# The first feed-forward of a hybrid encoder gets a group of seven products in its fourth chunk; row sums earlier, position tables and convolution diagonals later

## The chip, the cores and the metric

The kernel runs on one core of one Trainium2 chip. The metric is device time in microseconds from start to end of one execution, lower is better. The engines are named as in the profile: PE is TensorE's matmul, PEld its weight load, DVE VectorE, ACT ScalarE, POOL GpSimd, SP SyncE, which issues nearly all DMAs.

## The reference

Two layers over 256 tokens of width 1024, in float32. Each layer is half a feed-forward, a mixer, half a feed-forward; the mixer is a convolution module in layer 0 and latent attention in layer 1. At the end stands one more norm. So there are four feed-forwards, in this order: first (ahead of the convolution), second (behind it), third (ahead of the attention), fourth.

```python
def swiglu_ffn(h, w1, w3, w2):                      # 1024 -> 2816 -> 1024
    return (jax.nn.silu(h @ w1) * (h @ w3)) @ w2

for i in range(2):
    h = h + 0.5 * swiglu_ffn(rmsnorm(h, ffn_norm1[i]), ffn1_w1[i], ffn1_w3[i], ffn1_w2[i])
    m = rmsnorm(h, mix_norm[i])
    h = h + (conv_module(m, ...) if i == 0 else mla(m, positions, ...))
    h = h + 0.5 * swiglu_ffn(rmsnorm(h, ffn_norm2[i]), ffn2_w1[i], ffn2_w3[i], ffn2_w2[i])
return rmsnorm(h, final_norm)
```

Attention turns its keys and queries by `cos` and `sin` of position times frequency (the position tables). The convolution has 31 taps for each channel.

## The kernel before

**Precision.** A float32 product is made of three matmuls of a faster type: each operand is split into a high half (a cast, `hi`, on ACT) and a low half (the rest, `lo`, on DVE), and `mm3` (L330) adds high x low, high x high and low x high. In the profile these are L332, L335 and L336, named `u` in the first product of a feed-forward and `o` in the second.

**Weights.** All weights are cut into blocks of 128 x 2048 (1024 KB), in one list `blocks` in the order of use. `load` fetches a block into one of four `raw` buffers (SP queue), casts it in two pieces (L246) and makes its low half in two pieces (L247), into one of five `hi`/`lo` pairs. `load_ahead` runs up to three or four blocks ahead of the one in use. A `raw` buffer comes free when both low pieces are made, a `hi`/`lo` pair when TensorE has read it.

**A feed-forward** (`ffn_in`). The first product goes over 2816 columns in chunks `c` = 0 to 5: five of 512 columns, four blocks each (two for `w1`, two for `w3`), and one of 256 columns with two blocks. Two row tiles `tb` of 128 tokens, eight k tiles. After each chunk comes the activation and the multiplication (L953, L955), the result `s` is turned by a DMA through DRAM (`turn_blocks`, L475 to L484), and cast into `Gh` and `Gl` (L850). The second product goes over eleven blocks of `w2`.

**Groups of seven.** `seven_products` multiplies a 2 x 2 arrangement of blocks by seven products in place of eight, after Winograd: four blocks of weights become seven sums and differences, made on the way (`load_seven`: four subtractions of 128 x 2048 on DVE, L200; casts L214), and the rows need four sums too (`sums_of_rows`, L344; split by `forms_of`, L361 and L364). Where the rows are those of the normed input, `whole_rows` (L349) first adds their high and low halves into a tile `xs`, which takes a `raw` buffer. The products run in the order j = 0 to 6 into four PSUM banks; between them the banks are copied and added (L258): ACT copies bank `c11` to `c21` after product 0, and product 2 adds to `c21`.

`SEVEN_DOWN = (0, 1, 2, 3)`: the second product of all four feed-forwards begins with such a group. `SEVEN_UP = {1: (3,), 2: (3,), 3: (3,)}`: the first product of the second, third and fourth feed-forward has one in chunk 3. The row sums for it are made in chunk `min(seven_up) - 2`, or `- 1` where the rows come whole from the start (`X.whole`, only the first feed-forward, where it did not apply).

**The first feed-forward.** `first_rows` splits the input and the first two blocks as they arrive. The products of chunk 0 are L408. Beside it, `beside()` steps a generator `diagonals` that writes 63 convolution diagonals of 128 x 64 (`dpair`, and later `rows`, L1676) on ACT. The row sums' tile `rows4` is also used for the diagonals of the other half, which wait until the second product's row sums have been read.

**Position tables.** `rope_tables` (L1357 and on) makes them of 21 small operations on DVE and four sines on ACT. It is called late in the program, just ahead of the attention.

**Order.** A scheduler puts each engine's instructions in an order; `order(a, b)` makes a stand behind b on its engine with no wait, `urgent` raises a priority, `behind` keeps casts behind the last urgent instructions of their engine. What has no such tie the scheduler places by its own estimate: in the built kernel the position tables stand on DVE among chunk 1's blocks, and 31 diagonals on ACT stand there too. On each engine the instructions then run in that order.

**The norm ahead of the convolution** (`Plain`) loads the sigmoid's table on ACT (L666) ahead of the convolution's gates.

Of the kernel before, what the change touches and what calls it, by code (L numbers as in the profile page):

```python
# [19 lines left out]
P = 128  # L20
# [22 lines left out]
PIECES = 2  # L43
# [2 lines left out]

SEVEN_UP = {1: (3,), 2: (3,), 3: (3,)}
SEVEN_DOWN = (0, 1, 2, 3)  # L50

CONV_DVE = (0, 2, 4)
# [37 lines left out]
def trunk(ctx: ExitStack, tc: tile.TileContext, x, xt, first, pos, invf, gfin, wdw,  # L90
# [244 lines left out]
        nc.tensor.matmul(o, ah, bh, start=False, stop=False, skip_group_check=seeded)  # L335
        return nc.tensor.matmul(o, al, bh, start=False, stop=stop, skip_group_check=seeded)  # L336

    def sums_of_rows(x11, x12, x21, x22):


        sums = [(0, x22, x21, x22, ALU.add), (2, x21, x11, x21, ALU.subtract), (1, x11, x22, x11, ALU.subtract),
                (3, x12, x12, x11, ALU.subtract)]
        for n, out, left, right, op in sums:
            nc.vector.tensor_tensor(out, left, right, op=op)  # L344
        return sorted(((n, out) for n, out, *_ in sums), key=lambda s: s[0])

    def whole_rows(xh, xl):
# [20 lines left out]
    def seven_products(xh, xl, forms, banks, late={}):  # L368


        def rows(a, tb):
            k = slice(4 * a, 4 * a + 4)
            return xh[:, k, tbs(tb)], xl[:, k, tbs(tb)]

        def product(a, b, fresh):
            load_ahead(W_BUFS - 1)
            (hi, lo), = weights(1, False)
            for k in range(4):
                c = slice(k * 512, k * 512 + 512)
                before[:] = [mm3(b, a[0][:, k], a[1][:, k], hi[:, c], lo[:, c], fresh and k == 0, k == 3, before, True)]  # L380

        n0 = n_used[0]
        before = []
        c11, c21, c12, c22 = banks[0, 0], banks[1, 0], banks[0, 1], banks[1, 1]
        product(rows(0, 0), c11, True)
        first = urgent(nc.scalar.copy)(c21, c11)
        for cast in late.values():
            order(cast, first.ins)
        product(forms[0], c22, True)
        kept = tmp.tile([P, 512], F32, tag="s", name=uid("p5"))  # L390
        last = urgent(nc.scalar.copy)(kept, c22)
        product(forms[1], c21, False)
        add = urgent(nc.vector.tensor_add)(c12, c21, kept)
        order(casts[n0 + 5, 0][1], add.ins)
        for high, low in gates[-NT:] if not late else ():
            order(high, last.ins)
            order(low, add.ins)
        product(rows(1, 0), c11, False)
        product(forms[2], c21, False)
        add = urgent(nc.vector.tensor_add)(c22, c21, kept)  # L400
        order(casts[n0 + 6, 0][1], add.ins)
        product(forms[3], c12, False)
        product(rows(1, 1), c21, False)

# [245 lines left out]
    class Plain:  # L650
# [9 lines left out]
        @urgent  # L660
        def half(self, tb, i):
            sq = squares(self.ss[tb], h[tb], D, i)
            if tb == 0 and i == 1:
                self.sq = sq

                nc.scalar.activation(small.tile([P, 1], F32, tag="silu", name="sigm"), self.ss[0][:, 1:], AF.Sigmoid)  # L666

        @urgent
        def scale(self, tb):
# [159 lines left out]

    n_ffns = [0]  # L830
    gates = []

    def ffn(X, make_next, beside=lambda: None, apart=False):
        n = n_ffns[0]
# [4 lines left out]
    def ffn_in(act, X, make_next, beside, apart, seven_up, seven_down):  # L839
# [41 lines left out]
        for c in range(6):  # L881
# [4 lines left out]
            u = {}  # L886
            if c == 0 and X.pool:
                first_chunk(X, u)
            if seven_up and c == min(seven_up) - (1 if X.whole else 2):
                forms = forms_of(sums_of_rows(*whole_rows(X.xh, X.xl)), Gh[:, 14:], Gl[:, 14:])  # L890
            if c in seven_up:
                for key in ((0, 0), (0, 1), (1, 1), (1, 0)):
# [3 lines left out]
                beside()  # L896
            if both and seven_down:
                z11, z21, z12, z22 = (rows4[:, n, :] for n in range(4))
                down_sums = sums_of_rows(z11, z12, z21, z22)
                first_form = forms_of(down_sums[:1], *(act.tile([P, 2, S], F32R, tag=tag, name=uid(tag))  # L900
                                                       for tag in ("s1h", "s1l")))
            for m in range(0 if u else 1 if both else 2):
# [451 lines left out]
        return nxt  # L1354


    def rope_tables():  # L1357
        pi = const.tile([P, NT], I32, name="pi")
        fetch(pi, pos)
        fr = const.tile([P, 32], F32, name="fr")  # L1360
        fetch(fr, invf)
        pf = const.tile([P, NT], F32, name="pf")
        nc.vector.tensor_copy(pf, pi)
        ang = const.tile([P, NT, 32], F32, name="ang")
        for tb in range(NT):
            nc.vector.tensor_scalar(ang[:, tb, :], fr, pf[:, tb:tb + 1], None, op0=ALU.mult)
        a = ang.rearrange("p t f -> p (t f)")
        shape = [P, NT * 32]
        magic = 1.5 * 2.0 ** 23
        k = const.tile(shape, F32, name="turns")  # L1370
        nc.vector.tensor_scalar(k, a, 1.0 / (2 * math.pi), magic, op0=ALU.mult, op1=ALU.add)
        nc.vector.tensor_scalar(k, k, -magic, None, op0=ALU.add)
        kh = const.tile(shape, F32, name="turns_h")
        nc.vector.tensor_scalar(kh, k, 1.0 / 2048, magic, op0=ALU.mult, op1=ALU.add)
        nc.vector.tensor_scalar(kh, kh, -magic, 2048.0, op0=ALU.add, op1=ALU.mult)
        kl = const.tile(shape, F32, name="turns_l")
        nc.vector.tensor_sub(kl, k, kh)
        r = const.tile(shape, F32, name="red")
        nc.vector.tensor_copy(r, a)
        for p in _parts(2 * math.pi, 3, 12):  # L1380
            for kk in (kh, kl):
                nc.vector.scalar_tensor_tensor(r, kk, -p, r, op0=ALU.mult, op1=ALU.add)
        lim = 3.1415925
        nc.vector.tensor_scalar(r, r, -lim, lim, op0=ALU.max, op1=ALU.min)
        ra = const.tile(shape, F32, name="red_abs")
        nc.vector.tensor_scalar(ra, r, -1.0, None, op0=ALU.mult)
        nc.vector.tensor_max(ra, ra, r)
        nc.vector.tensor_scalar(ra, ra, -1.0, math.pi / 2, op0=ALU.mult, op1=ALU.add)

        cc = const.tile([P, NT, 2, 32], F32, name="cc")  # L1390
        sn = const.tile([P, NT, 2, 32], F32, name="sn")
        r3 = r.rearrange("p (t f) -> p t f", f=32)
        ra3 = ra.rearrange("p (t f) -> p t f", f=32)
        for i in range(2):
            nc.scalar.activation(cc[:, :, i, :], ra3, AF.Sin)
        nc.scalar.activation(sn[:, :, 0, :], r3, AF.Sin, scale=-1.0)
        nc.scalar.activation(sn[:, :, 1, :], r3, AF.Sin)
        return cc, sn

    def rope(pool, dst, src, n, cc, sn, tb, after=()):  # L1400

# [266 lines left out]
    def diagonals():  # L1668
# [4 lines left out]
        nc.gpsimd.tensor_tensor(ident2, ident[:, :64], ident[:, 64:], op=ALU.add)  # L1673
        for g in (1, 0):
            for j in range(KP - g):
                nc.scalar.activation(dpair[g][:, j, :], ident2, AF.Copy, scale=wp2[:, g, j:j + 1])  # L1676
                if j % 4 == 3:
                    yield
            if g == 1:

                while "down" not in stage:
                    yield
        nc.scalar.activation(ident2, ident2, AF.Copy, scale=wp2[:, 1, KP - 1:])

    class Rows512:

# [6 lines left out]
    rows = Rows512()  # L1693

    stage = []
    todo = diagonals()

    def beside():
# [10 lines left out]
    apart.close()  # L1709
    X = ffn(X, lambda act: Norm("ffn1_1", half=True, turn_by_dma=rows), apart=True)  # L1710
    X = ffn(X, lambda act: Norm("mix_1", turn_by_dma=rows), apart=True)
    cc, sn = rope_tables()
    X = mla(X, lambda act: Norm("ffn2_1", half=True, turn_by_dma=rows), cc, sn)
    ffn(X, Final)

# [100 lines left out]
```

## Time and profile before

| | us |
|---|---|
| median of 3 runs | 897.50 |
| lowest, highest | 896.81, 900.43 |
| the profiled execution | 897.52 |
| its span in the profile | 895.7 |
| PE busy, PEld busy | 887.9, 745.7 |
| DVE busy, ACT busy, POOL busy | 743.6, 571.8, 105.2 |
| granted clock of TensorE | 0.999 |

The profiled execution's own time is 1.8 us over its span; the rest lies ahead of the first and behind the last instruction. Times in the trace count from the start of the span. The first feed-forward's first product lies between 5.7 and 125.4 us, its second product ends at some 183 us. A row of a group ends with busy time, mean length of one in ns, and the idle time of its engine just before, with what ended it. A row of the timeline begins with start and length in us. Matmuls overlap, so their lengths are more than their distance.

### The profile page before, as it was taken

What the parts mean: (1) busy time and instruction counts of PE and PEld (TensorE: products, weight loads), DVE (VectorE), ACT (ScalarE), POOL (GpSimd) and SP (SyncE); (2) the same over time, 40 slices, a digit from 0 to 9 for tenths busy, and PEclk for the clock granted to TensorE, in tenths of its full rate; (3) what the DMA queues carried; (4) which work ended last, traced back from release to release, by engine and by line L of the source; (5) the groups of instructions that cost most, each with busy time, mean ns of one, the idle gap of its engine ahead of it and who ended that gap; (6) DMA issues with size and microseconds to landing.
All of it is one profiled execution on the core that took longest, in us unless ns stands there. A gap on an engine that the chain in (4) does not pass through costs nothing.

```text
span 895.7 us, 12244 instructions
## 1 busy us (share of the span) xinstructions
PE 887.9 (99%) x4221; PEld 745.7 (83%) x4221; DVE 743.6 (83%) x1083; ACT 571.8 (64%) x993; POOL 105.2 (12%) x227
## 2 busy tenths in 40 slices
PE   9999999999999999999999999999999999999997
PEld 7888888898988888888888888888899888888886
DVE  6787779579998999999598989995768579999973
ACT  7966458488876646656375566673677566474762
POOL 1000000079962000000010000001400010000000
PEclk9999999999999999999999999999999999999999
DMA  9997629834215864939759369396635449387551
GB/s 336 354 341 252 229 59 367 296 124 165 95 60 193 291 257 147 386 97 372 271 177 340 113 221 350 114 387 202 219 142 189 141 147 345 107 285 291 165 210 48
DMA packets 71054, 198.94 MB, mean 222 GB/s; under 512 B 12368, under 2 KB 41936, under 8 KB 51664
## 3 DMA queue, kind: packets, MB, share of 16 engines
q1 hardware_dynamic: 70560, 197.47, 61.9%
q8 instruction: 33, 0.54, 0.2%
q10 hardware_dynamic: 432, 0.69, 0.2%
q14 instruction: 29, 0.24, 0.1%
HBM read 181.87 MB, written 16.25 MB: 221 GB/s over the span
## 4 chain that ended last, share of the span: by engine, by line
PE 78%; DVE 10%; DMA 8%; issue 2%; SPq 1%; ACT 1%; POOL 0%; DVEq 0%; ACTq 0%
PE u L332 10%; PE u L336 10%; PE u L335 10%; PE o L336 9%; PE o L332 9%; PE o L335 9%; PE u L1002 3%; PE gate L1002 3%; DVE lo L247 3%; DMA gd<-gt 2%; PE u L408 2%; DVE lo L200 2%; DMA raw<-in_f2w 1%; DMA rows<-gd 1%; DMA hd<-rows 1%
## 5 line engine op out<-in xcount | busy, mean ns | idle before, releaser
L247 DVE TENSOR_TENSOR lo<-raw,hi 128x1024 fp32r<-128x1024 f32 (+1 forms) x236 | 276.0, 1210 | 39.0 <-ACT hi L246 37.7
L246 ACT CAST hi<-raw 128x1024 fp32r<-128x1024 f32 (+1 forms) x238 | 236.7, 1044 | 86.1 <-DMA raw<-in_f2w 28.0
L332 PE MATMUL u<-lo,Xh 128*128 128x512 f32 x612 | 238.7, 390 | 0.3
L335 PE MATMUL u<-hi,Xh 128*128 128x512 f32 x612 | 238.2, 389 | 0.0
L336 PE MATMUL u<-hi,Xl 128*128 128x512 f32 x612 | 237.9, 389 | 0.0
L332 PEld LDWEIGHTS u<-lo,Xh 128*128 128x128 f32 x612 | 114.9, 188 | 25.9 <-DVE lo L200 1.6
L336 PEld LDWEIGHTS u<-hi,Xl 128*128 128x128 f32 x612 | 114.9, 188 | 24.6 <-DVE Xl L462 0.5
L335 PEld LDWEIGHTS u<-hi,Xh 128*128 128x128 f32 x612 | 114.9, 188 | 23.7
L214 ACT CAST hi<-raw 128x1024 fp32r<-128x1024 f32 x98 | 97.6, 1049 | 54.2 <-DVE raw L200 47.5
L200 DVE TENSOR_TENSOR lo<-raw,hi 128x1024 fp32r<-128x1024 f32 x98 | 115.9, 1216 | 5.5 <-ACT hi L214 5.3
L332 PE MATMUL o<-lo,Gh 128*128 128x512 f32 (+1 forms) x276 | 106.6, 386 | 0.0
L335 PE MATMUL o<-hi,Gh 128*128 128x512 f32 (+1 forms) x276 | 106.5, 386 | 0.0
L336 PE MATMUL o<-hi,Gl 128*128 128x512 f32 (+1 forms) x276 | 106.5, 386 | 0.0
L434 POOL TENSOR_TENSOR ms<-ss 128x1 f32<-128x1 f32 x16 | 8.1, 511 | 598.2 <-ACT junk L426 598.2
L200 DVE TENSOR_TENSOR raw<-raw,raw 128x2048 f32<-128x2048 f32 x28 | 63.8, 2278 | 1.7 <-DMA raw<-in_f2w 1.4
L335 PEld LDWEIGHTS o<-hi,Gh 128*128 128x128 f32 x276 | 51.8, 188 | 10.5
L336 PEld LDWEIGHTS o<-hi,Gl 128*128 128x128 f32 x276 | 51.8, 188 | 10.5
L332 PEld LDWEIGHTS o<-lo,Gh 128*128 128x128 f32 x276 | 51.8, 188 | 10.4
L1091 DVE SCALAR_TENSOR_TENSOR acc<-V,dw,acc 128x128 f32<-128x128 f32 (+1 forms) x174 | 53.9, 389 | 0.0
L953 ACT ACTIVATE s<-u,R 128x512 f32<-128x512 f32 (+1 forms) x48 | 30.9, 647 | 26.9 <-PE u L336 26.2
L1112 ACT ACTIVATE prod<-V,dw 128x128 f32<-128x128 f32 (+1 forms) x128 | 45.8, 416 | 2.0 <-POOL Y L1113 1.0
L794 DVE SCALAR_TENSOR_TENSOR h<-o,rh,h 128x512 f32<-128x512 f32 (+1 forms) x18 | 12.9, 718 | 29.0 <-PE o L336 29.0
(265 smaller groups left out, 1260.2 us busy)
## 6 DMA issues: line engine op xcount, KB each, us to landing
raw<-in_f2w SPq DMA_DIRECT2D x66, 1024.0 KB, 6.5
raw<-in_f1w SPq DMA_DIRECT2D x62, 1024.0 KB, 6.6
raw<-in_cw SPq DMA_DIRECT2D x12, 1024.0 KB, 4.9
gd<-gt SPq DMA_DIRECT2D x160, 64.0 KB, 2.9
gb<-gd SPq DMA_DIRECT2D x24, 256.0 KB, 2.9
rows<-gd SPq DMA_DIRECT2D x16, 256.0 KB, 4.1
raw<-in_wo SPq DMA_DIRECT2D x4, 1024.0 KB, 4.9
hd<-rows SPq DMA_DIRECT2D x56, 64.0 KB, 2.4
```

The costliest lines, as they stand in the source:

```text
L200: ins = nc.vector.tensor_sub(out, left, right)
L214: casts[n, i] = nc.scalar.copy(hi[:, c], raw[:, c]), sub(lo[:, c], raw[:, c], hi[:, c].bitcast(F32))
L246: casts[len(loaded), i] = (nc.scalar.copy(hi[:, c], raw[:, c]), low.tensor_sub(lo[:, c], raw[:, c], hi[:, c].bitcast(F32)))
L247: low.tensor_sub(lo[:, c], raw[:, c], hi[:, c].bitcast(F32)))
L332: mm = nc.tensor.matmul(o, ah, bl, start=start, stop=False, skip_group_check=seeded)
L335: nc.tensor.matmul(o, ah, bh, start=False, stop=False, skip_group_check=seeded)
L336: return nc.tensor.matmul(o, al, bh, start=False, stop=stop, skip_group_check=seeded)
L408: mm = nc.tensor.matmul(o, al if kind == "x" else ah, bl if kind == "l" else bh, start=start and n == 0, stop=stop and n == len(kinds) - 1)
L953: nc.scalar.activation(s[:, :w], u[0, tb][:, :w], AF.Silu, scale=X.r[tb])
L1002: mm = nc.tensor.matmul(u[:, t], w[:, c], X.x[:, k, t], start=(k == 0), stop=(k == KT - 1))
L1091: dve_last.append(nc.vector.scalar_tensor_tensor(out if j == j1 - 1 else y, v, w, y, op0=ALU.mult, op1=ALU.add))
L1112: prods_last.append(nc.scalar.activation(p, v, AF.Copy, scale=w))
```

## The change

- The first feed-forward gets a group of seven in chunk 3 of its first product: `SEVEN_UP` has an entry for it. Its four blocks are no longer multiplied by 96 matmuls of 512 columns but by seven products of twelve.
- Its row sums are made in chunk 1, as in the three others; the exception for `X.whole` is gone.
- In `seven_products`, the low half of the second of the last chunk's two gates (L850) stands behind the last low piece of the group's last block, in all four feed-forwards. In the first feed-forward the row sums for the second product stand behind that piece too (`seven_last`).
- The diagonals of the first half (31 and one) each stand behind the cast of the block loaded last when they are made, so they are spread over the chunks.
- The position tables are made at the end of the generator `diagonals`, behind the last cast of the block after the one in use, and the sigmoid's table load stands behind the last sine.

```diff
@@ -46,7 +46,7 @@
 
 
 
-SEVEN_UP = {1: (3,), 2: (3,), 3: (3,)}
+SEVEN_UP = {0: (3,), 1: (3,), 2: (3,), 3: (3,)}
 SEVEN_DOWN = (0, 1, 2, 3)
 
 CONV_DVE = (0, 2, 4)
@@ -335,13 +335,15 @@
         nc.tensor.matmul(o, ah, bh, start=False, stop=False, skip_group_check=seeded)
         return nc.tensor.matmul(o, al, bh, start=False, stop=stop, skip_group_check=seeded)
 
-    def sums_of_rows(x11, x12, x21, x22):
+    def sums_of_rows(x11, x12, x21, x22, first=None):
 
 
         sums = [(0, x22, x21, x22, ALU.add), (2, x21, x11, x21, ALU.subtract), (1, x11, x22, x11, ALU.subtract),
                 (3, x12, x12, x11, ALU.subtract)]
         for n, out, left, right, op in sums:
-            nc.vector.tensor_tensor(out, left, right, op=op)
+            ins = nc.vector.tensor_tensor(out, left, right, op=op)
+            if first is not None:
+                order(ins, first.ins)
         return sorted(((n, out) for n, out, *_ in sums), key=lambda s: s[0])
 
     def whole_rows(xh, xl):
@@ -395,10 +397,14 @@
         for high, low in gates[-NT:] if not late else ():
             order(high, last.ins)
             order(low, add.ins)
+        low_gates = [low for high, low in gates[-NT:] if not late]
         product(rows(1, 0), c11, False)
         product(forms[2], c21, False)
         add = urgent(nc.vector.tensor_add)(c22, c21, kept)
         order(casts[n0 + 6, 0][1], add.ins)
+        seven_last.append(casts[n0 + 6, PIECES - 1][1])
+        for low in low_gates[1:]:
+            order(low, seven_last[-1].ins)
         product(forms[3], c12, False)
         product(rows(1, 1), c21, False)
 
@@ -663,7 +669,9 @@
             if tb == 0 and i == 1:
                 self.sq = sq
 
-                nc.scalar.activation(small.tile([P, 1], F32, tag="silu", name="sigm"), self.ss[0][:, 1:], AF.Sigmoid)
+                table = nc.scalar.activation(small.tile([P, 1], F32, tag="silu", name="sigm"), self.ss[0][:, 1:],
+                                             AF.Sigmoid)
+                order(table, tables[-1].ins)
 
         @urgent
         def scale(self, tb):
@@ -829,6 +837,7 @@
 
     n_ffns = [0]
     gates = []
+    seven_last = []
 
     def ffn(X, make_next, beside=lambda: None, apart=False):
         n = n_ffns[0]
@@ -886,7 +895,7 @@
             u = {}
             if c == 0 and X.pool:
                 first_chunk(X, u)
-            if seven_up and c == min(seven_up) - (1 if X.whole else 2):
+            if seven_up and c == min(seven_up) - 2:
                 forms = forms_of(sums_of_rows(*whole_rows(X.xh, X.xl)), Gh[:, 14:], Gl[:, 14:])
             if c in seven_up:
                 for key in ((0, 0), (0, 1), (1, 1), (1, 0)):
@@ -896,7 +905,7 @@
                 beside()
             if both and seven_down:
                 z11, z21, z12, z22 = (rows4[:, n, :] for n in range(4))
-                down_sums = sums_of_rows(z11, z12, z21, z22)
+                down_sums = sums_of_rows(z11, z12, z21, z22, seven_last[-1] if X.whole else None)
                 first_form = forms_of(down_sums[:1], *(act.tile([P, 2, S], F32R, tag=tag, name=uid(tag))
                                                        for tag in ("s1h", "s1l")))
             for m in range(0 if u else 1 if both else 2):
@@ -1354,13 +1363,13 @@
         return nxt
 
 
-    def rope_tables():
+    def rope_tables(first):
         pi = const.tile([P, NT], I32, name="pi")
         fetch(pi, pos)
         fr = const.tile([P, 32], F32, name="fr")
         fetch(fr, invf)
         pf = const.tile([P, NT], F32, name="pf")
-        nc.vector.tensor_copy(pf, pi)
+        order(nc.vector.tensor_copy(pf, pi), first.ins)
         ang = const.tile([P, NT, 32], F32, name="ang")
         for tb in range(NT):
             nc.vector.tensor_scalar(ang[:, tb, :], fr, pf[:, tb:tb + 1], None, op0=ALU.mult)
@@ -1394,8 +1403,7 @@
         for i in range(2):
             nc.scalar.activation(cc[:, :, i, :], ra3, AF.Sin)
         nc.scalar.activation(sn[:, :, 0, :], r3, AF.Sin, scale=-1.0)
-        nc.scalar.activation(sn[:, :, 1, :], r3, AF.Sin)
-        return cc, sn
+        return cc, sn, nc.scalar.activation(sn[:, :, 1, :], r3, AF.Sin)
 
     def rope(pool, dst, src, n, cc, sn, tb, after=()):
 
@@ -1673,7 +1681,9 @@
         nc.gpsimd.tensor_tensor(ident2, ident[:, :64], ident[:, 64:], op=ALU.add)
         for g in (1, 0):
             for j in range(KP - g):
-                nc.scalar.activation(dpair[g][:, j, :], ident2, AF.Copy, scale=wp2[:, g, j:j + 1])
+                diagonal = nc.scalar.activation(dpair[g][:, j, :], ident2, AF.Copy, scale=wp2[:, g, j:j + 1])
+                if g == 1:
+                    order(diagonal, casts[len(loaded) - 1, PIECES - 1][0].ins)
                 if j % 4 == 3:
                     yield
             if g == 1:
@@ -1681,6 +1691,8 @@
                 while "down" not in stage:
                     yield
         nc.scalar.activation(ident2, ident2, AF.Copy, scale=wp2[:, 1, KP - 1:])
+        yield
+        tables.extend(rope_tables(casts[n_used[0] + 1, PIECES - 1][1]))
 
     class Rows512:
 
@@ -1693,6 +1705,7 @@
     rows = Rows512()
 
     stage = []
+    tables = []
     todo = diagonals()
 
     def beside():
@@ -1709,7 +1722,7 @@
     apart.close()
     X = ffn(X, lambda act: Norm("ffn1_1", half=True, turn_by_dma=rows), apart=True)
     X = ffn(X, lambda act: Norm("mix_1", turn_by_dma=rows), apart=True)
-    cc, sn = rope_tables()
+    cc, sn, _ = tables
     X = mla(X, lambda act: Norm("ffn2_1", half=True, turn_by_dma=rows), cc, sn)
     ffn(X, Final)
```

## The prediction

> **What bounds the kernel now.** I read the page first (busy times, the clock, the chain that ended last), then what TensorE waited for, then its timeline, then the stretches.
>
> ```profile
> span 895.7 us, 12244 instructions
> PE 887.9 (99%) x4221; PEld 745.7 (83%) x4221; DVE 743.6 (83%) x1083; ACT 571.8 (64%) x993; POOL 105.2 (12%) x227
> PE 78%; DVE 10%; DMA 8%; issue 2%; SPq 1%; ACT 1%; POOL 0%; DVEq 0%; ACTq 0%
> PE warm L324 <- DVE still L319: 1.0, 1, 1.0
> PE rb L1148 <- POOL rc L1144: 0.4, 1, 0.4
> 59.91 0.39 PE L336 MATMUL u<-hi,Xl 128*128 128x512 f32 x1
> 62.63 0.39 PE L336 MATMUL u<-hi,Xl 128*128 128x512 f32 x1
> 22.00:132.00 110.00, 110.00 (x487) 91.06 (x487) 85.99 (x109) 71.15 (x124) 1.44 (x6) 1.00 0.72 253
> 22.00:44.00 22.00, 22.00 (x98) 18.22 (x98) 17.63 (x35) 20.04 (x48) 1.44 (x6) 1.00 0.98 354
> ```
>
> TensorE is busy for 99% of the span, and the view of its waits has just two rows, 1.4 us in all. A busy row alone could hide slack, since matmuls overlap: one lasts 0.39 us. Their starts say more. Between 59.91 and 62.63 lie twelve matmuls, so one starts every 2.72/12 = 0.227 us, and a stretch without waits can get shorter only by having fewer of them. The last two rows are stretches of the first feed-forward (busy time in the order PE, PEld, DVE, ACT, POOL; then clock, DMA share, GB/s). From 22 to 132 us TensorE never stops, DVE works 86.0 of 110 us and ACT 71.2; from 22 to 44 the DMA engines are 98% busy. Two things can therefore happen: fewer matmuls, or a TensorE that begins to wait because the 24 us in which DVE is idle there are used up, or because something comes in the wrong order.
>
> **What the change takes away.** Chunk 3's four weight blocks take 2 products x 2 row tiles x 8 k x 3 = 96 matmuls; seven products of 4 x 3 take 84. The built order of the changed kernel confirms twelve fewer TensorE rows. Those are the twelve between the two rows above: **-2.72 us**. By the Trainium skill ("TensorE: Matmul & The Clock Gate", Part 1) a warm 512-column matmul starts 215.7 ns after the last, which would make it 2.59; this trace has 227, and that decides.
>
> **What it adds, and whether it fits.**
>
> ```profile
> L247 DVE TENSOR_TENSOR lo<-raw,hi 128x1024 fp32r<-128x1024 f32 x60 | 70.9, 1218 | 21.6 <-ACT hi L246 21.3
> L214 ACT CAST hi<-raw 128x1024 fp32r<-128x1024 f32 x14 | 13.9, 1047 | 9.9 <-DVE raw L200 9.9
> L200 DVE TENSOR_TENSOR raw<-raw,raw 128x2048 f32<-128x2048 f32 x4 | 9.1, 2284 | 0.1
> L344 DVE TENSOR_TENSOR rows<-rows 128x512 f32<-128x512 f32 x4 | 2.7, 673 | 0.0
> L364 DVE TENSOR_TENSOR rows<-rows,rows 128x512 fp32r<-128x512 f32 x3 | 2.0, 690 | 3.5 <-ACT rows L361 3.5
> L1382 DVE SCALAR_TENSOR_TENSOR red<-turns_l,red 128x64 f32<-128x64 f32 x4 | 0.9, 224 | 0.1
> 730.71 2.28 DVE xs L349
> ```
>
> DVE gets: one sum of the input's halves (2.28, a row of another feed-forward), four row sums (4 x 0.67), four low halves of them (4 x 0.69), four subtractions of whole blocks (4 x 2.28), the low halves of three more blocks (6 x 1.22) and two additions (2 x 0.69, a row further down): 2.28 + 2.69 + 2.76 + 9.14 + 7.31 + 1.38 = 25.6 us. The twenty-one small operations of the position tables, some 21 x 0.22 = 4.6 us, leave this stretch. Room 24.0 + 4.6 = 28.6, need 25.6: it fits on the whole with 3 us over, so it is the places that decide. I see five: four where TensorE may begin to wait, and one where it stops waiting.
>
> **Place 1, the second block of chunk 1.** The input sum and row sums are now queued on DVE right behind the fourth block's low half.
>
> ```profile
> 25.53 1.23 DVE L247 TENSOR_TENSOR lo<-raw,hi 128x1024 fp32r<-128x1024 f32 x1 [5.00 <-ACT hi L246]
> 29.61 2.34 DVE L247 TENSOR_TENSOR lo<-raw,hi 128x1024 fp32r<-128x1024 f32 x2
> 27.49 0.39 PE L332 MATMUL u<-lo,Xh 128*128 128x512 f32 x1
> 32.93 0.39 PE L332 MATMUL u<-lo,Xh 128*128 128x512 f32 x1
> ```
>
> DVE stands idle for the 5.00 us ahead of 25.53, until the next block is cast. The sum, four row sums and one low half (2.28 + 2.69 + 0.69 = 5.66) fill that and reach 26.2, so the next block's first low half ends at some 27.4, due at 27.49: just in time. Three more low halves (2.1) and the 0.66 already late move the block behind it from 29.61 to some 32.3 with its transposition between; its first half ends 0.1 to 0.7 us behind its due time of 32.93. I take **+0.3** (0 to 0.9).
>
> **Place 2, the new group of seven.**
>
> ```profile
> 56.00 4.63 DVE L247 TENSOR_TENSOR lo<-raw,hi 128x1024 fp32r<-128x1024 f32 x4
> 71.01 0.39 PE L332 MATMUL u<-lo,Xh 128*128 128x512 f32 x1
> ```
>
> TensorE starts chunk 3 at 71.01; its first block's low half starts at 56.00. The seventh product is due 6 x 2.72 later, at 87.3: DVE has 31.3 us for seven blocks (7 x 2.32, from the 4.63 for two), four subtractions (9.1), one or two additions (1.4), the four gate halves, two multiplications and two transpositions that lie there (8 x 0.68 = 5.4): 32.2 us. The second half of the last block is due six matmuls later (1.36), so this ends about level. The block after the group is fetched late too, as its buffers are held by the four blocks. I take **+0.5** for group and block (0 to 1.5).
>
> **Place 2b, the same group in the three other feed-forwards.** The change ties one gate's low half behind the last block there too.
>
> ```profile
> 354.70 0.68 DVE L850 TENSOR_TENSOR Gl<-gb,Gh 128x512 fp32r<-128x512 f32 x1
> 355.31 0.69 DVE L258 TENSOR_TENSOR u<-u,p 128x512 f32<-128x512 f32 x1
> 355.91 2.35 DVE L200 TENSOR_TENSOR lo<-raw,hi 128x1024 fp32r<-128x1024 f32 x2
> 357.17 0.50 PE u L332
> 531.80 0.50 PE u L332
> 796.73 0.50 PE u L332
> ```
>
> In the chain each of the three groups has one TensorE step of 0.50 where a matmul takes 0.23, so each loses 0.27, waiting for the low half that starts at 355.91. The gate's low half (0.61 from start to start) goes from ahead of it to behind it; that is more than the 0.27, so the wait goes: **-0.8** (-0.8 to 0; what is late next is the following block, whose pieces come behind the same amount of work as before). In the second product's groups of these three, a subtraction of 2.28 now goes ahead of two low halves. I cost that at nothing: the chain has no TensorE step above 0.23 there, and the lead of the sixth product hides it; without that lead it would be up to 2.28 each.
>
> **Place 3, the group of the second product.** This is the largest. The seeding copy of the third product (L258) stands on ACT behind the convolution's diagonals.
>
> ```profile
> 125.41 0.39 PE L332 MATMUL o<-lo,Gh 128*128 128x512 f32 x1
> 125.39 0.62 ACT L361 CAST rows<-rows 128x512 fp32r<-128x512 f32 x1 [2.02 <-PE u L335]
> 125.91 0.47 ACT L953 ACTIVATE s<-u,R 128x256 f32<-128x256 f32 x1
> 126.77 2.02 ACT L1676 ACTIVATE rows<-dpair,wpair 128x64 f32<-128x64 f32 x8 [0.38 <-DVE rows L364]
> 128.70 0.57 ACT L258 COPY o<-o 128x512 f32<-128x512 f32 x1
> 136.20 2.27 ACT L1676 ACTIVATE rows<-dpair,wpair 128x64 f32<-128x64 f32 x9
> 138.37 1.98 ACT L214 CAST hi<-raw 128x1024 fp32r<-128x1024 f32 x2
> 140.11 2.35 DVE L200 TENSOR_TENSOR lo<-raw,hi 128x1024 fp32r<-128x1024 f32 x2
> ```
>
> The group begins at 125.41; the copy is due two products later, 5.44 after that. Before, ACT had cast the third and fourth blocks ahead, and the copy ended 129.27, 3.9 after the start. In the built order of the changed kernel the four casts come between: row cast, activation, four casts, eight diagonals, copy. From the start: 0.5 + 0.5, four casts at 0.95 (two took 1.98 at 138.37), eight diagonals 1.93, copy 0.57: 7.3 us, and TensorE waits 7.3 - 5.4 = **+1.8** (1.0 to 2.3; a late subtraction on DVE would add, and casts that start before the group would save).
>
> **Place 4, the last product of that group.** Sixteen diagonals now stand in one piece ahead of its casts, where nine did: 16 x 0.25 = 4.0 for 2.27. Copy, two row casts, two pairs of casts, a copy and these end 16.4 after the group's start; a cast (1.05) and a low half (1.2) later it is 18.7, due at 6 x 2.72 + 1.8 = 18.1. I take **+0.5** (0 to 1.0).
>
> **Moved at no cost.** The tables now lie among the last blocks of the second product, where DVE idles 3.08 us between block casts:
>
> ```profile
> 172.94 2.36 DVE L247 TENSOR_TENSOR lo<-raw,hi 128x1024 fp32r<-128x1024 f32 x2 [3.08 <-ACT hi L246]
> ```
>
> Two such holes hold their 4.6 us. Without that cover the sigmoid's table load on ACT, which now waits for the last sine, would come later and the convolution's first gate with it, at most by 4.6. The fetches for tables and diagonals stand on SP where they stood; SP's fetches of weights are one buffer later, which is rival 2. POOL has the same order.
>
> **Sum.** Against the profiled execution's 897.52: -2.72 - 0.8 + 0.3 + 0.5 + 1.8 + 0.5 = -0.4, so **897.1 us**. The median of the runs shown is 897.50, practically the same execution; its runs lie from 896.8 to 900.4, so I call anything within 0.5% (4.5 us) no change that can be measured. Lower ends of the places: -0.8 + 0 + 0 + 1.0 + 0 gives 895.0; upper ends: 0 + 0.9 + 1.5 + 2.3 + 1.0 gives 900.5.
>
> **Rivals.**
> 1. *All is hidden*, and the three others gain: 897.5 - 2.72 - 0.8 = 894.0. For it: the other feed-forwards have both groups and lose 0.27 at one place. Against: they have no diagonals ahead of the copy. 0.15.
> 2. *The start starves* (slower). The row sums take one of four fetch buffers from 20.5 to some 32 us, so the eighth block is fetched not at 20.80 but when the fifth is split, and each fetch after it goes a place back:
>
> ```profile
> 20.80 8.05 SPq L238 DMA_DIRECT2D raw<-in_f1w  x2
> ```
>
> The two fetches here lie almost 8 us apart. A block is 1024 KB, 3.0 us at the 354 GB/s of the stretch above. If one is lost, the queue refills it from requests that waited anyway; if two are lost on a queue that is 98% busy, 5.9 us of lead go, and place 2 has none to spare: 897.1 + 5.9 = 903.0. It moves the time past 0.5% from a loss of 4.9 us before 56 us. 0.10.
> 3. *The wait at place 3 cools the array.* The first matmuls run slow:
>
> ```profile
> 1.04 4.66 PE warm L324 x21
> ```
>
> 256 columns in 4.66/21 = 0.222 us is half the later rate. Were the clock to fall back for as long again, 2.3 us would be lost: 899.4. Nothing in this trace's later rows shows it, and 1.8 us is short. 0.02. The Trainium skill (same page, Part 1) wants an idle window of about 3.4 us before the clock halves; by that rule it does not happen here, and no gap of this trace is long enough to test it.
> 4. *The change does not do what it says.* The built order has the twelve fewer matmuls: 0.
>
> **Numbers.** The forecast 0.68, rival 1 0.15, rival 2 0.10, rival 3 0.02, and 0.05 for what is named nowhere, half of it to each side. The range of 8 in 10 leaves out rival 2 and half of rival 1 and reaches to the upper ends: 894.4 to 900.5. The forecast and rivals 1 and 3 are within 4.5 us: same 0.87. Slower takes most of rival 2 and some of the unnamed, 0.10. Faster by 4.5 us would need more than the 3.5 that the matmuls and place 2b are worth: 0.03.
>
> **What would show it.** In the profile after: 4209 TensorE matmuls; TensorE waiting on ACT at the third product of the second group, for 1 to 2 us, with the copy behind casts and diagonals; a step near 0.7 for 0.23 around the end of the first group and its next block; DVE without its 5 us hole at 20.5; no step of 0.50 in the groups of the three others. It would be wrong if TensorE's waits in the first 190 us sum to under 1.3 or over 5.7 us, or if the convolution's first product starts more than 1.5 us earlier or 3 us later than before.

## The result: slower by 0.3%, and the profile after

The changed kernel takes 900.55 us in the median of 11 runs (899.21 to 902.92), before 897.50. The ratio is 1.0031, with a 95% interval of 1.0021 to 1.0040; measured once more beside the experiments it was 1.0050 (1.0031 to 1.0069). One of before's eleven runs took 989.38 us; the ratios are taken over the fast runs and are not the quotient of two medians. The forecast was 897.1 and 894.4 to 900.5: 3.5 us too low, and the range missed by 0.05. The profiled execution took 900.55, as the median.

The head of the page and the view of TensorE's waits, after (columns of the second: total in us, times, longest):

```profile
span 898.7 us, 12252 instructions
PE 887.0 (99%) x4209; PEld 744.7 (83%) x4209; DVE 767.1 (85%) x1104; ACT 580.6 (65%) x1005; POOL 106.7 (12%) x227
PE u L332 <- DVE lo L247: 2.5, 2, 2.2
PE o L332 <- ACT o L258: 1.6, 1, 1.6
PE warm L324 <- DVE still L319: 1.0, 1, 1.0
PE u L332 <- DVE lo L200: 0.4, 1, 0.4
PE o L332 <- DVE lo L200: 0.2, 1, 0.2
```

Twelve matmuls are gone, as forecast, yet the busy time fell by only 0.9 us for their 2.72, and the waits grew from 1.4 to 5.7 us. One of them is 2.2 long, on the low half of the fifth block, chunk 1's first: place 1, for which the forecast had 0.3. Its surroundings, in TensorE's timeline:

```profile
27.17 0.39 PE L414 MATMUL u<-hi,Xl 128*128 128x512 f32 x1
29.77 0.79 PE L332 MATMUL u<-lo,Xh 128*128 128x512 f32 x1 [2.21 <-DVE lo L247]
30.36 0.63 PE L335 MATMUL u<-hi,Xh 128*128 128x512 f32 x1
32.91 0.43 PE L335 MATMUL u<-hi,Xh 128*128 128x512 f32 x1
```

The fifth block's first product starts 2.60 us behind the last of chunk 0, where 0.23 is the rule: 2.37 lost. From 30.36 to 32.91 lie six steps of 0.425, nearly twice the warm distance. From 29.77 to 32.91 there are seven matmuls in 3.14 us instead of 1.59, another 1.55. That is 3.9 us in one place. The stretches around it show the granted clock (the number ahead of the DMA share):

```profile
26.17:29.58 3.41, 1.39 (x7) 0.80 (x5) 2.30 (x3) 3.41 (x6) 0.16 (x1) 1.00 0.42 139
29.58:32.99 3.41, 3.23 (x8) 2.55 (x9) 3.41 (x6) 3.41 (x6) 0.00 (x0) 0.50 0.19 29
```

The sum comes out: waits 5.7 - 1.4 = +4.3, half clock +1.55, matmuls -2.72, together +3.1; the span grew by 3.0. Comparing each matmul's start with that of the same matmul before says where. After is 0.1 us ahead at the end of chunk 0. Place 1 costs 4.0 up to 33 us, place 2 costs 0.55, place 3 1.9 and place 4 0.5; less 2.72, after is 4.15 late when the convolution begins. It regains 1.1 between 255 and 300 us: 0.7 where before's execution waits for GpSimd (L1148), as the edited kernels of experiments 2, 3, 6 and 12 do too, and 0.4 in small steps. So the first feed-forward loses more than the 3.0 of the span, and part of what comes back may be chance.

Why the fifth block is late, from three timelines, GpSimd (POOL), ScalarE (ACT), VectorE (DVE). Before:

```profile
20.92 0.19 POOL L434 TENSOR_TENSOR ms<-ss 128x1 f32<-128x1 f32 x1 [16.06 <-ACT junk L426]
21.48 0.57 POOL L437 TENSOR_TENSOR R<-ms,neghalf 128x1 f32<-128x1 f32 x1
22.08 0.69 ACT L953 ACTIVATE s<-u,R 128x512 f32<-128x512 f32 x1
24.45 2.00 ACT L246 CAST hi<-raw 128x1024 fp32r<-128x1024 f32 x2 [0.25 <-DMA raw<-in_f1w]
```

After:

```profile
20.37 2.29 DVE L351 TENSOR_TENSOR xs<-Xh,Xl 128x2048 f32<-128x2048 f32 x1
22.70 2.15 DVE L344 TENSOR_TENSOR xs<-xs 128x512 f32<-128x512 f32 x3
20.72 2.00 POOL L440 TENSOR_TENSOR ms<-ss 128x1 f32<-128x1 f32 x1 [16.00 <-ACT junk L432]
23.52 1.02 POOL L443 TENSOR_TENSOR R<-ms,neghalf 128x1 f32<-128x1 f32 x1
24.58 0.69 ACT L962 ACTIVATE s<-u,R 128x512 f32<-128x512 f32 x1 [2.60 <-POOL R L443]
26.64 0.61 ACT L363 CAST Gh<-xs 128x512 fp32r<-128x512 f32 x1
27.15 1.99 ACT L246 CAST hi<-raw 128x1024 fp32r<-128x1024 f32 x2
27.28 0.69 DVE L366 TENSOR_TENSOR Gl<-xs,Gh 128x512 fp32r<-128x512 f32 x1 [2.44 <-ACT Gh L363]
28.49 1.22 DVE L247 TENSOR_TENSOR lo<-raw,hi 128x1024 fp32r<-128x1024 f32 x1
```

The VectorE work came as priced: 2.29 for the sum, 2.15 for three row sums, done at 24.85, and then VectorE stands idle for 2.44 us. What is late is GpSimd. Its first operation on 128 x 1 numbers takes 2.00 us for 0.19 and ends at 22.72, just behind the end of the sum at 22.66; the power takes 1.02 for 0.57. So the first activation starts 2.5 us later, and the fifth block's cast, which stands on ScalarE behind both activations and a row cast, starts at 27.15 for 24.45. The Trainium skill ("SBUF — State Buffer", section "Who interferes with whom") says that a VectorE instruction with two inputs in SBUF contends with a GpSimd instruction that reads SBUF, for a pair of ports that it calls an exclusive lock. The trace agrees: GpSimd's operation begins inside the sum and ends 0.06 us behind it. Experiment 1 tests it.

### The profile page after: what moved, and what is told of

Its sections match the earlier page's. It is cut to its first block, busy times and chain, and to the rows that moved or that the text cites. A ratio compares the mean times of both kernels' runs of the same rounds, so it can differ in the third digit from the quotient of the medians.

```text
span 898.7 us, 12252 instructions
## 1 busy us (share of the span) xinstructions
PE 887.0 (99%) x4209; PEld 744.7 (83%) x4209; DVE 767.1 (85%) x1104; ACT 580.6 (65%) x1005; POOL 106.7 (12%) x227
## 4 chain that ended last, share of the span: by engine, by line
PE 81%; DMA 7%; DVE 6%; ACT 4%; issue 1%; SPq 1%; POOL 1%; DVEq 0%; ACTq 0%
PE u L332 13%; PE u L335 13%; PE u L336 13%; PE o L332 9%; PE o L335 9%; PE o L336 9%; PE u L1011 3%; PE gate L1011 3%; DVE lo L247 2%; DMA raw<-in_f2w 2%; DMA gd<-gt 1%; DVE lo L200 1%; ACT hi L214 1%; DMA h<-in_x 1%; PE tp L449 1%
## 5 line engine op out<-in xcount | busy, mean ns | idle before, releaser
L247 DVE TENSOR_TENSOR lo<-raw,hi 128x1024 fp32r<-128x1024 f32 (+1 forms) x228 | 266.9, 1214 | 23.9 <-ACT hi L246 22.5
L246 ACT CAST hi<-raw 128x1024 fp32r<-128x1024 f32 (+1 forms) x230 | 228.6, 1044 | 71.5 <-DMA raw<-in_f2w 27.4
L332 PE MATMUL u<-lo,Xh 128*128 128x512 f32 x592 | 231.8, 392 | 2.9 <-DVE lo L247 2.5
L336 PE MATMUL u<-hi,Xl 128*128 128x512 f32 x592 | 231.2, 391 | 0.0
L335 PE MATMUL u<-hi,Xh 128*128 128x512 f32 x592 | 231.1, 390 | 0.0
L214 ACT CAST hi<-raw 128x1024 fp32r<-128x1024 f32 x112 | 111.6, 1048 | 44.1 <-DVE raw L200 35.8
L200 DVE TENSOR_TENSOR lo<-raw,hi 128x1024 fp32r<-128x1024 f32 x112 | 132.3, 1216 | 7.4 <-ACT hi L214 7.2
L332 PEld LDWEIGHTS u<-lo,Xh 128*128 128x128 f32 x592 | 111.6, 188 | 27.5 <-DVE lo L247 3.6
L336 PEld LDWEIGHTS u<-hi,Xl 128*128 128x128 f32 x592 | 111.5, 188 | 23.6 <-DVE Xl L468 0.4
L200 DVE TENSOR_TENSOR raw<-raw,raw 128x2048 f32<-128x2048 f32 x32 | 73.1, 2285 | 2.5 <-DMA raw<-in_f2w 1.8
```

What stands on the lines that cost most here:

```text
L200: ins = nc.vector.tensor_sub(out, left, right)
L214: casts[n, i] = nc.scalar.copy(hi[:, c], raw[:, c]), sub(lo[:, c], raw[:, c], hi[:, c].bitcast(F32))
L246: casts[len(loaded), i] = (nc.scalar.copy(hi[:, c], raw[:, c]), low.tensor_sub(lo[:, c], raw[:, c], hi[:, c].bitcast(F32)))
L247: low.tensor_sub(lo[:, c], raw[:, c], hi[:, c].bitcast(F32)))
L332: mm = nc.tensor.matmul(o, ah, bl, start=start, stop=False, skip_group_check=seeded)
```

## Experiments

Each is an edit of the changed kernel. Theory A: the sum's second input holds GpSimd, which makes the fifth block late (2.4 us), and the array cools (1.6 us); places 3 and 4 are as forecast. Ratios are against before, with 95% intervals; after was 1.0031. The runs were made in three rounds, each with before beside it: 1 to 4 (before's median 897.46), 5 and 8 to 10 (898.15), 6, 7, 11 and 12 (897.81). Across rounds, compare ratios and not medians.

| | median us | ratio |
|---|---|---|
| 1 one input | 897.41 | 1.0001 (0.9992 to 1.0010) |
| 2 sum behind the fifth block | 896.51 | 0.9998 (0.9988 to 1.0009) |
| 3 sums in chunk 2 | 898.48 | 1.0017 (1.0002 to 1.0032) |
| 4 sixteen matmuls in the wait | 898.61 | 1.0020 (1.0012 to 1.0028) |
| 5 five matmuls in the wait | 899.56 | 1.0021 (1.0013 to 1.0030) |
| 6 block's casts first | 897.91 | 1.0004 (0.9996 to 1.0013) |
| 7 after again | 901.65 | 1.0050 (1.0031 to 1.0069) |
| 8 diagonals behind the group | 901.32 | 1.0031 (1.0017 to 1.0046) |
| 9 no group | 896.86 | 0.9990 (0.9982 to 0.9999) |
| 10 sum two blocks later, diagonals | 898.08 | 0.9997 (0.9984 to 1.0011) |
| 11 sum (as 2) and diagonals | 896.97 | 0.9992 (0.9981 to 1.0004) |
| 12 casts first (as 6) and diagonals | 898.71 | 1.0008 (0.9998 to 1.0018) |

**1. An instruction of the same length with one input.**

```diff
-        nc.vector.tensor_add(x, xh.bitcast(F32), xl.bitcast(F32))
+        if n_used[0] == 4:
+            total = small.tile([P, 1], F32, tag="silu", name=uid("total"))
+            nc.vector.tensor_scalar(x, xh.bitcast(F32), 1.0, None, op0=ALU.mult, op1=ALU.add, accum_out=total)
+        else:
+            nc.vector.tensor_add(x, xh.bitcast(F32), xl.bitcast(F32))
```

It leaves the low halves out of the first feed-forward's row sums.

> Kernel after, with one VectorE instruction changed at its place: the 128x2048 sum of two tiles becomes a scaling of one tile by 1.0 with an accumulator, 128x2048 from one input, so that the low halves are left out of the row sums. Every queue has the same order, VectorE about the same busy time, the fetch buffer is held as long. Theory A: with one input GpSimd isn't kept waiting: its first operation is 0.2 us for 2.0, the first activation starts near 22.1 for 24.6, the wait at 27.2 falls from 2.4 to under 0.9 (the four row sums, 0.67 each with two inputs, can still hold the second power) and the half clock goes: 896.6 to 897.6. Rivals B (queue) and D (buffer): nothing changes, wait 2.4, 900.5.

VectorE, GpSimd and TensorE in its timeline:

```profile
20.85 2.29 DVE L353 TENSOR_SCALAR_CACHE_REDUCE xs<-Xh 128x2048 f32<-128x2048 f32 x1
21.21 0.19 POOL L444 TENSOR_TENSOR ms<-ss 128x1 f32<-128x1 f32 x1 [16.60 <-ACT junk L436]
23.18 1.13 POOL L447 TENSOR_TENSOR R<-ms,neghalf 128x1 f32<-128x1 f32 x1
27.49 0.39 PE L418 MATMUL u<-hi,Xl 128*128 128x512 f32 x1
28.06 0.50 PE L332 MATMUL u<-lo,Xh 128*128 128x512 f32 x1 [0.18 <-DVE lo L247]
```

This bears the mechanism out. The instruction is another one (a scaling with an accumulator), but it is as long (2.29), stands at the same place and holds the same buffer; it has one input, and GpSimd's operation in the middle of it takes 0.19 again. That the number of inputs decides, and not the kind of instruction, fits the row sums: the power of the second row tile falls beside them, they still have two inputs, and it takes 1.13. TensorE's wait shrinks to 0.57 - 0.23 = 0.34, the half clock is gone, and so is the whole loss: 1.0031 becomes 1.0001. The rivals of queue and buffer expected no change. The lack of a fetch buffer, rival 2 of the prediction, is thus no part of it.

**2. The sum behind the fifth block.**

```diff
-        nc.vector.tensor_add(x, xh.bitcast(F32), xl.bitcast(F32))
+        add = nc.vector.tensor_add(x, xh.bitcast(F32), xl.bitcast(F32))
+        if n_used[0] == 4:
+            order(add, casts[4, PIECES - 1][1].ins)
```

> Kernel after, with the sum of the input's halves still in chunk 1 but ordered on VectorE behind the fifth block's last low half. Theory A: GpSimd's first operation is back from 2.0 us to 0.2, no wait at 27.2, no stretch at half clock. The sum now stands ahead of the sixth block, whose slack was 2.1 us for 2.3 of sum: 0 to 0.5 there. 896.6 to 897.2. Rival B expects the same. Rival D (the fetch buffer that the sum's tile holds starves the start): the buffer is held even longer, so 900 or more.

```profile
21.03 0.19 POOL L442 TENSOR_TENSOR ms<-ss 128x1 f32<-128x1 f32 x1 [16.74 <-ACT junk L434]
PE u L332 <- DVE lo L247: 1.4, 3, 0.5
```

GpSimd is back at 0.19. In place of one wait there are three of at most 0.5 (the profiled execution, at 898.60, is one of the longer ones: the input's second half landed 1.4 us late there). The median, 896.51, is at the lower end of what was expected (896.6 to 897.2).

**3. The row sums a chunk later**, where the kernel before would have had them.

```diff
-            if seven_up and c == min(seven_up) - 2:
+            if seven_up and c == min(seven_up) - (1 if X.whole else 2):
```

> Kernel after, with the first feed-forward's row sums put back one chunk later (chunk 2); all else stays. Theory A (port and clock): in chunk 1 the 128x2048 sum of the input's halves on VectorE holds the path that GpSimd reads through, the norm's three GpSimd operations end 2.5 us later, both activations on ScalarE with them, the fifth block's cast behind these, and TensorE waits 2.4 us at 27.2; then the array runs at half clock for 3 us, 1.6 us more. With the sums a chunk later both go: 3.9 less than 900.55, so 896.6 (up to 897.3 if the group in chunk 3 then waits). Rival B (queue): the 5.7 us of added VectorE work alone makes the fifth block late; it expects the same here. Rival C: the first chunk costs little and the loss is at the second product's group; then 899.5 or more stays.

Half a miss: 898.48 for 896.6 to 897.3. The first wait is gone, but the profiled execution has another, at the third product of the new group, on the copy that seeds it; its runs spread from 895.7 to 903.9. From the view of waits, the timelines of ScalarE and VectorE, and the stretches:

```profile
PE u L332 <- ACT u L258: 3.8, 1, 3.8
70.73 0.62 ACT L859 CAST Gh<-rows 128x512 fp32r<-128x512 f32 x1 [4.07 <-DMA rows<-gd]
72.59 2.28 DVE L200 TENSOR_TENSOR raw<-raw,raw 128x2048 f32<-128x2048 f32 x1
74.96 2.00 ACT L214 CAST hi<-raw 128x1024 fp32r<-128x1024 f32 x2 [3.61 <-DVE raw L200]
79.71 0.57 ACT L258 COPY u<-u 128x512 f32<-128x512 f32 x1
79.07:82.48 3.41, 2.14 (x5) 1.76 (x6) 3.39 (x4) 3.41 (x5) 0.00 (x0) 0.50 0.56 140
```

A subtraction of blocks now stands on VectorE behind the low half of turned rows, whose DMA landed late; the block's cast waits for the subtraction, and the copy stands behind that cast, four diagonals and the next cast. In after the same subtraction starts at 65.62, ahead of those rows. The wait also halves the clock, for two stretches of 3.41 us in place of one: TensorE is busy for 0.88 us of the stretch ahead of 79.07, the one from 79.07 is at half clock, and so is the next, to 85.90.

**4 and 5. Matmuls on zeros in the wait.**

```diff
+            if X.whole and c == 1:
+                keep_warm(16, "B", mm)
```

> Kernel after, with sixteen TensorE matmuls of 256 columns on zeros (as at the kernel's start) put between chunk 0 and chunk 1, into the wait at 27.2. The wait stays. Theory A: the slow matmuls behind it, 0.43 us apart from 29.8 to 32.9, are the clock, halved by the idle time; with 1.8 us of the 2.4 filled the clock stays whole and 1.6 us go: 899.0. Rival E: these matmuls are slow for another reason (operands that come late, or traffic): 900.5 stays.

> As with the sixteen matmuls on zeros in the wait at 27.2, but five: 0.57 us of work and then some 1.8 us of waiting, as long as the 1.76 at 132.4 behind which no matmul was slow. If the length of the idle stretch decides, the clock stays whole: 899.0. If any wait of this size at this place cools the array, 900.5.

Sixteen, in TensorE's timeline:

```profile
27.37 1.92 PE L324 MATMUL warm<-still 128*128 128x256 bf16 x16
29.82 0.50 PE L332 MATMUL u<-lo,Xh 128*128 128x512 f32 x1 [0.53 <-DVE lo L247]
30.16 0.40 PE L335 MATMUL u<-hi,Xh 128*128 128x512 f32 x1
30.39 0.40 PE L336 MATMUL u<-hi,Xl 128*128 128x512 f32 x1
```

The real product starts as late as in after, and behind it the step is 0.23 again (30.16 to 30.39): the slow matmuls were the clock. With five the profile shows no slow matmul either. The ratios are 0.0011 and 0.0010 below after's, some 1 us of 897 where 1.6 was expected, and their intervals overlap after's (1.0021 to 1.0040). So the profiles show what the slow matmuls were, and the times don't settle what they cost on the whole; in run 7 place 1 does not cool at all.

**6. The block's casts ahead of the activations.** The port is left as it is.

```diff
+            if n_used[0] == 4:
+                order(cast, casts[4, PIECES - 1][0].ins)
+                order(sub, casts[4, PIECES - 1][1].ins)
...
+                if X.whole and c == 0:
+                    order(silu, casts[4, PIECES - 1][0].ins)
```

> Kernel after, with the sum of the input's halves where it is, but on ScalarE the two activations of chunk 0 and the four row casts stand behind the fifth block's casts, and on VectorE the rows' low halves behind its low halves. Theory A, in two steps: the port still holds GpSimd, whose first operation stays at 2.0 us; but the fifth block no longer waits behind the activations, so the wait at 27.2 goes down to 0 to 0.5 and the half clock with it: 896.6 to 897.4. Rival B (the added VectorE work alone): the sum and the row sums still stand ahead of the low half, wait 1 or more, 898.5 or more.

```profile
21.26 2.00 POOL L443 TENSOR_TENSOR ms<-ss 128x1 f32<-128x1 f32 x1 [16.83 <-ACT junk L435]
PE u L332 <- DVE lo L247: 1.3, 2, 1.0
```

GpSimd still takes 2.00, and the fifth block is in time all the same. The wait is 1.0 long and comes one block later, more than the 0 to 0.5 expected, and the median is 0.5 above the 896.6 to 897.4 expected; nothing cools. So most of the loss needed both: GpSimd held, and the block's cast queued behind what waits for GpSimd.

**7. After once more.**

> Kernel after itself, once more, on the chip of the three others. In the run with the diagonals ordered behind the group TensorE waited 2.8 us at 27.0 and no matmul behind it was slow. Theory A1 (a wait of 2.4 to 2.8 us halves the clock in every execution): the profile shows the slow matmuls again, times as before, 899.2 to 902.9. Theory A2 (it depends on where the wait falls against something that runs by itself): times in two groups some 1.6 us apart, with or without slow matmuls in the profile.

The stretches below are counted back from the change of clock at 134.28 in steps of 3.413 us. The trace's record of the granted clock begins at 4.57 us here and changes at 134.28 and 137.69, which is 38 steps and one. In after's first profile it begins at 5.69 and changes at 29.58 and 32.99, seven steps and one.

```profile
25.05:28.46 3.41, 2.57 (x12) 1.80 (x10) 0.97 (x3) 2.58 (x4) 1.45 (x5) 1.00 0.85 324
28.46:31.88 3.42, 1.60 (x7) 1.35 (x8) 3.42 (x6) 3.42 (x6) 0.00 (x0) 1.00 0.03 7
130.87:134.28 3.41, 1.34 (x7) 0.77 (x5) 3.08 (x3) 3.41 (x11) 0.00 (x0) 1.00 0.19 39
134.28:137.69 3.41, 3.41 (x8) 2.77 (x9) 2.73 (x4) 3.41 (x6) 0.00 (x0) 0.50 0.00 0
PE u L332 <- DVE lo L247: 2.9, 2, 2.7
PE o L332 <- ACT o L258: 2.4, 2, 2.1
```

Here the wait at place 1 is 2.7 long and cools nothing, while the 2.1 at place 3 halves the clock. The first is cut by a border of these stretches, so that TensorE is busy for 1.60 us or more in each; the second lies within one, busy for 1.34. In after's first profile the wait lay within one stretch too (1.39 above). In the profiles theory A2 holds: what a wait of this size costs depends on where it falls. Its times in two groups did not show: the six runs lie at 898.60, 900.53, 901.34, 901.95, 903.93 and 905.65.

**8. The second half's diagonals behind the group's last cast.**

```diff
+        seven_cast.append(casts[n0 + 6, PIECES - 1][0])
...
+                else:
+                    order(diagonal, seven_cast[-1].ins)
```

> Kernel after, with the second half's diagonals on ScalarE ordered behind the last cast of the second product's group of seven; all else stays. Theory A: the waits at the third and the last product of that group (1.76 and 0.34 at 132.4 and 145.2) go, 2.0 us: 900.55 becomes 898.5; the first chunk keeps its 3.9. Rival F (something else is late next, the subtractions on VectorE): at most half goes, 899.5 or more.

```profile
PE o L332 <- DVE lo L200: 0.4, 1, 0.4
PE o L332 <- DVE lo L247: 0.2, 1, 0.2
```

These are the waits between 120 and 190 us. The one on the copy (1.6) is gone, and two on VectorE's low halves sum to 0.6, where after has 0.2: 1.2 us less in the profile, with rival F partly right. The time does not show it (1.0031, as after; 901.32 us for the 898.5 expected), so what this cure is worth in time stays open.

**9. All but the group.**

```diff
-SEVEN_UP = {0: (3,), 1: (3,), 2: (3,), 3: (3,)}
+SEVEN_UP = {1: (3,), 2: (3,), 3: (3,)}
...
-                down_sums = sums_of_rows(z11, z12, z21, z22, seven_last[-1] if X.whole else None)
+                down_sums = sums_of_rows(z11, z12, z21, z22, seven_last[-1] if X.whole and seven_up else None)
```

> Kernel after without the first feed-forward's group of seven and its row sums (the entry taken out again): the later position tables, the spread diagonals and the gate's low half alone. Theory A: 4221 matmuls, no wait in the first chunk, tables and diagonals cost nothing, the gate's tie gives 0.3 to 0.8: 896.7 to 897.2, so that the group as made costs 3.4 to 3.9 net of its own 2.7. Rival G (the moves cost): 898.5 or more.

Tables, diagonals and the gate's tie give 0.0010 (0.0001 to 0.0018), 0.9 us, as forecast for place 2b (0.8). By the starts of the same matmuls, the three groups of place 2b gain 0.38, 0.39 and 0.27 us on before, 1.0 in all. Besides the kernel's start the view of waits has only one of 0.2 (on ACT, L601), and no group has one. So the group as made costs 1.0031/0.9990, some 3.7 us (5.4 by run 7's 1.0050), in spite of its twelve matmuls less.

**10 to 12. Cures together**, the diff of 8 with three ways for the first chunk: in 10 the sum stands behind the seventh block (`casts[6, PIECES - 1]` in the diff of 2), in 11 behind the fifth, in 12 the diff of 6.

> Both cures in the kernel after: the sum of the input's halves on VectorE behind the seventh block's last low half (still chunk 1), and the second half's diagonals behind the group's last cast. Theory A: 3.9 and 2.0 go: 900.55 becomes 894.6, and with the sum a block later than in the run before none of the 0.5 at the sixth block stays. Against before's 897.5: the 2.72 of twelve matmuls and two of three gate waits, less some 0.5 at the block after the first group. Rival D (the buffer): the sum holds its buffer to some 50 us, so the fetches run late: 896 or more.

> Two cures together: the sum behind the fifth block's last low half (as in the run that gave 896.5) and the second half's diagonals behind the last cast of the second product's group (which took 1.2 out of that group's waits). Theory A: the two add up, 895.3, ratio near 0.9978 against before. Rival H (the group in chunk 3 has no lead left, so that what is won ahead of it is lost at its third product, as in the two runs with the sum later still): 897 or more, with a wait at 76.

> The other cure of the first chunk (casts of the fifth block first) with the diagonals behind the group's last cast. Theory A: 896.6 to 897.4 less 1.2: 895.4 to 896.2, and no wait at 76, since the row sums are made early. Rival H: 897 or more, with a wait at 76.

The longest wait of 10, then that of 11, the kernel's start apart:

```profile
PE u L332 <- ACT u L258: 1.6, 1, 1.6
PE u L332 <- DVE lo L247: 0.5, 1, 0.5
```

All three missed theory A: 898.08 for 894.6, 896.97 for 895.3, 898.71 for 895.4 to 896.2. In 10 the wait of experiment 3 is back, shorter, as rival H has it. In 11 nothing above 0.5 is left in the profile, and its execution took 895.65, near the 895.3; but the median is 896.97, the interval reaches 1, and what the longer runs lose stays open. In 12 there is no wait at 76, against rival H, and the one on the sixth block stays (0.9). No version beats before by an amount that these measurements can tell; 9, which has no group, is the one whose interval stays below 1.

## Why the prediction was wrong, point by point

- **Matmuls.** Right: 4209, and after gains 2.72 us on before between 60 and 92 us.
- **Place 1.** The step that failed: 3.9 us for +0.3. The fifth block's first low half was to end at some 27.4, just in time, with the 0.3 on the block behind it; it ended at 29.71 (28.49 + 1.22). That the time came out only 0.05 us above the range is no near hit, since this one term was off by 3.6. Its VectorE prices were right, and with GpSimd left free (experiment 1) the wait is 0.34, inside the 0 to 0.9. Two things were not looked at. The sum fills a hole in which GpSimd had been working for the activations; "POOL has the same order" was true, and its times were not. And the block's low half was taken to wait for VectorE alone, while its cast stands on ScalarE behind what GpSimd releases.
- **Place 2.** Right: the block behind the first group starts 0.64 us behind the matmul ahead of it (93.75 to 94.39), where 0.23 is the rule, and after loses 0.55 there, for +0.5. The group itself does not wait.
- **Place 2b.** Right in experiment 9. In after's profile two of the three steps are gone, and the second feed-forward's group has a wait of 0.4 on another low half (L200); of the other executions only experiment 2's has one like it, 0.3 in the fourth feed-forward.
- **Place 3.** Right: a wait of 1.6, 1.9 lost by the matmuls' starts, for +1.8, with the queue as worked out:

```profile
128.03 3.89 ACT L214 CAST hi<-raw 128x1024 fp32r<-128x1024 f32 x4
131.82 2.01 ACT L1684 ACTIVATE rows<-dpair,wpair 128x64 f32<-128x64 f32 x8
133.74 0.58 ACT L258 COPY o<-o 128x512 f32<-128x512 f32 x1
```

- **Place 4.** Right: a wait of 0.2, 0.5 lost by the matmuls' starts, for +0.5.
- **Rival 2.** Experiment 1 keeps the buffer held and loses nothing.
- **Rival 3.** The mechanism came, with a chance of 0.02: at place 1 in one execution, at place 3 in another, for 1.55 us each. The step that failed was to read "an idle window of about 3.4 us" as a wait of that length. The Trainium skill ("TensorE: Matmul & The Clock Gate", Part 1) says that the window runs on by itself. The runs agree with its length (3.41 us at half clock in both executions, twice that in experiment 3's); but it need not be idle throughout: busy for 1.39 or 1.34 us of 3.41 was little enough, 1.60 was not. So a wait of 2.4 us cools or not by where it falls.
- **The marks.** The waits in the first 190 us sum to 5.3 (the view's 5.7 less the 0.4 of the second feed-forward), under the 5.7 set as wrong. Of the other signs, the wait on ACT and the step near 0.7 came; VectorE's hole moved, to 2.44 us ahead of 27.28, in place of going. The last mark told it: the convolution's first product, in the two chains, starts 4.15 us later, where over 3 was wrong.

```profile
183.59 1.78 PE gate L1002 x16
187.74 1.78 PE gate L1011 x16
```

## What to carry to other kernels

Work that fills a hole on VectorE is not free because VectorE was idle: if it reads two SBUF tiles, look at what GpSimd does in that hole, and who waits for it. Follow a block's chain over all engines it passes (fetch, cast, low half), and place long two-input instructions behind the small GpSimd work on the path. And price a TensorE wait of 2 us or more at its length plus, in some executions, one or two windows of 3.41 us at half clock.

## What the hardware showed unexpectedly

- A GpSimd operation on 128 x 1 numbers took 2.00 us for 0.19 beside a two-input VectorE instruction of 2.29, and 0.19 beside a one-input instruction of the same length.
- The granted clock changed on borders that fit steps of 3.41 us. It fell behind stretches in which TensorE was busy for 0.88, 1.34 and 1.39 us, and did not behind one of 1.60. The last matmuls of the kernel narrow this down: it fell behind a stretch with 1.48 us busy (experiment 11) and not behind one with 1.58 (experiment 1). What decides in between stays open.
- Once halved, the clock stayed so behind a stretch in which TensorE was busy for 2.14 of 3.41 us (experiment 3), and rose behind one with 3.23 (after).
